# Seven-product matmuls kept to three of the six sections of a QKV projection, and twelve attention heads gathered in the other two late sections

## The chip, the cores and the metric

The kernel runs on one core of one Trainium2 chip. The metric is the device time of one execution in microseconds (us). The engines are TensorE (PE; its weight loads are shown apart as PEld), VectorE (DVE), ScalarE (ACT), GpSimd (POOL) and SyncE (SP, which issues most of the DMAs). Each engine takes its instructions strictly in the order in which they were written, and waits at one of them until what it needs is there.

## The reference

One decoder layer (DEPTH is 1) on 256 tokens of width 2048: attention with 16 heads of 128, a SwiGLU of inner width 5632, and a layer norm after each. The mixer of layer 0 is block-sparse, but with 256 tokens there is a single block of 256, so every query sees its own block alone: causal attention with a relative-position bias.

```python
def moba_mixer(x, w_qkv, w_o, rel_bias):
    q, k, v = jnp.split(x @ w_qkv, 3, axis=-1)          # 2048 -> 3 * 2048
    q, k, v = heads(q) * HEAD_DIM ** -0.5, heads(k), heads(v)
    o = moba_attention(q, k, v, rel_bias.T)              # one block: causal softmax(q k + bias) v
    return o @ w_o

def reference(...):
    x = layer_norm(ALPHA * x + moba_mixer(...), ln1_g, ln1_b)
    return layer_norm(ALPHA * x + (silu(x @ w_gate) * (x @ w_up)) @ w_down, ln2_g, ln2_b)
```

All of it is float32.

## The kernel before

**Three matmuls for one product.** Every operand is split into a high and a low part (`split`: ACT copies the high part in the fp32r format, DVE subtracts it from the source for the low part), and each product of a 128x128 by a 128x512 tile is three matmuls: high by high, high by low, low by high. Weights come from DRAM in pieces of 128 x 1024 floats (two K tiles by 512 columns, 512 KB) and are split as they arrive.

**Sections, pairs, blocks.** Each large matrix product is cut into sections of two chunks of 512 output columns. A section has 8 pairs of K tiles, and each pair is two blocks. The input projection has six sections, q0 to q5 (`QKV`); then come o0 and o1 (the attention's output projection), f0 to f10 (gate and up) and d (down). A plain pair takes two K tiles, two row halves of the tokens and two chunks: eight products, 24 matmuls, in two blocks of 12. In a section that has `comb` set, three of the eight pairs (`ST`: 1, 3, 5) are done with seven products of sums and differences in Strassen's manner: 21 matmuls, in blocks of 9 and 12. For that the weights' sums are made (`quad_sums`: four DVE additions of 128x512 for each pair) and 3.5 pieces instead of 2 are split, and differences of the two token halves (`combine_x`, tiles `xC`) stand as left operands.

**PSUM.** There are 8 banks of 128x512, handed out by a queue: `bank` takes the one that has been free longest, `give` puts a bank back. A section with `comb` holds seven sums (`acc` 1 to 7) and leaves one bank free while it runs; a plain section holds four and leaves four. At a section's end `sums_1` to `sums_3` (seven DVE operations and one of ACT) bring the seven sums together; a plain section's four are copied out.

**Attention.** One head is five steps, each put behind a block. `at_t1` transposes q and k on PE into a bank and splits them; `at_s` multiplies them into a bank, DVE adds the bias and takes the maximum (lines 453, 455), and ACT takes exponentials; `at_n` divides by the sums (reciprocal on DVE, two scalings on ACT, lines 470 and 471); `at_t2` transposes the probabilities into a bank and splits them, and splits the head's v; `at_o` multiplies by v into a bank and ACT copies the result. Heads come in four groups of four. Groups 0 to 2 run beside the projection, group 3 beside o0. Of groups 0 and 1 the result goes to DRAM (`od`) and is loaded again before the output projection (`load_o`, `split_o`).

**Order.** Nothing is scheduled: a loop writes the blocks one by one, loads and splits of a pair three to five blocks ahead of it, and before or after each block whatever `before(t, ...)` and `after(t, ...)` have put there. The six sections before are (q, k of group 0), (v of groups 0, 1), (q, k of 1), (q, k of 2), (v of 2, 3), (q, k of 3); all but q0 have `comb`. The first step of head 0 stands behind the first block of q2, each head starts 5 blocks after the one ahead of it, and its steps stand 0, 3, 6, 9 and 12 blocks behind its start, so that twelve heads spread over the 64 blocks of q2 to q5.

Of the kernel before, what the change touches and what calls it, by code (L numbers as in the profile page):

```python
# [13 lines left out]
AF = mybir.ActivationFunctionType  # L14
OP = mybir.AluOpType

P = 128
# [19 lines left out]
SKEW_D = 3  # L37
AHEAD = 3
AHEAD_Q = 5
QKV = (((0, 0), (1, 0)), ((2, 0), (2, 1)), ((0, 1), (1, 1)), ((0, 2), (1, 2)), ((2, 2), (2, 3)), ((0, 3), (1, 3)))  # L40
SQK, SV = {0: 0, 1: 2, 2: 3, 3: 5}, {1: (0, 1), 4: (2, 3)}
KEEP = 2
ST = (1, 3, 5)
WARM = 9
# [5 lines left out]
def decoder_layer(ctx: ExitStack, tc: tile.TileContext, x, xt, rel_bias, w_qkv, w_o, g1, b1, gb1,  # L50
                  w_gate, w_up, w_down, g2, b2, c_ident, c_hot, c_mask, out):
    nc = tc.nc
# [7 lines left out]
    def p4(shape, dt, name):  # L60
        return sb.tile(shape, dt, tag="p4", bufs=P4, name=name)

    def s2(shape, dt, name):
        return sb.tile(shape, dt, tag="s2", bufs=S2, name=name)

    def tiny(shape, name):
        return sb.tile(shape, F, tag="tiny", bufs=16, name=name)
# [3 lines left out]
    def bank(name):  # L71
        n = free.popleft()
        t = ps.tile([P, CW], F, tag=f"b{n}", bufs=1, name=name)
        held[id(t)] = (t, n)
        return t

    def give(*ts):
        for t in ts:
            free.append(held.pop(id(t))[1])
# [4 lines left out]
    def split(hi, lo, src):  # L84
        nc.scalar.activation(hi, src, AF.Copy)  # L85
        nc.vector.tensor_tensor(lo, src, f32(hi), op=OP.subtract)  # L86
# [83 lines left out]
    def h_lhs(kt, m):  # L170
# [1 line left out]
        return hi[:, kt % 4, m * P:(m + 1) * P], lo[:, kt % 4, m * P:(m + 1) * P]  # L172

    xC, x1C = {}, {}
    Q = [Sec(f"q{n}", [(w_qkv, 4 * i + g) for i, g in pair], 8, x_lhs, xC if n else None)
         for n, pair in enumerate(QKV)]
    WO = [Sec(f"o{i}", [(w_o, 2 * i + c) for c in range(2)], 8, o_lhs) for i in range(2)]
    NF = FF // CW
# [5 lines left out]
    def add(sec, pairs, m, chunks=None, ks=(0, 1)):  # L184
        blocks.append((sec, pairs, m, range(len(sec.chunks)) if chunks is None else chunks, ks))
        return len(blocks) - 1

    def alternate(sec, a, b):
        for p in range(a, b):
            add(sec, [p], 0)  # L190
            add(sec, [p], 1)

    for k in range(2):
        for m in range(2):
            add(Q[0], [0], m, ks=[k])
    alternate(Q[0], 1, 8)
    for s in Q[1:]:
        alternate(s, 0, 8)
    alternate(WO[0], 0, 8)
    k = 8 - SKEW_WO  # L200
# [6 lines left out]
    k = DN.npair - SKEW_D  # L207
# [7 lines left out]
    first, last = {}, {}  # L215
# [15 lines left out]
    order = []  # L231
    for s in [*Q, *WO, *FU, DN]:
        for p in range(s.npair):
            if s is Q[0] and not p:
                continue
            f = first[s.name, p]
            if s.comb is None:
                todo = [(start[s.name, p], "plain")]
            elif p in ST:
                a = 4 if s in Q or (s is FU[1] and p == 1) else 6  # L240
                todo = [(f - a, "sums"), (f - a + 1, "raw"), (f - a + 2, "low")]
# [137 lines left out]
    grp = {}  # L379

    def new_qk(g):
        grp[g] = {n: p4([P, 2, CW], F, f"{n}{g}") for n in "qk"}
        return grp[g]

    def first_qk(m):
        t = new_qk(0) if m == 0 else grp[0]
        nc.scalar.activation(t["q"][:, m, :], Q[0].acc[m, 0], AF.Copy)
        nc.vector.tensor_copy(t["k"][:, m, :], Q[0].acc[m, 1])
        give(Q[0].acc[m, 0], Q[0].acc[m, 1])


    def sums_1(s, t):
# [36 lines left out]
    att = {}  # L429
# [35 lines left out]
    def at_n(h):  # L465
        sc, sm = att[h]
        rs = tiny([P, 2], "rs")
        nc.vector.tensor_scalar(rs, sm, 1e-30, None, op0=OP.max)
        nc.vector.reciprocal(rs, rs)
        nc.scalar.activation(sc[:, :2 * P], sc[:, :2 * P], AF.Identity, scale=rs[:, 0:1])  # L470
        nc.scalar.activation(sc[:, 2 * P:], sc[:, 2 * P:], AF.Identity, scale=rs[:, 1:2])

    def at_t2(h):
        sc, _ = att[h]
        b = bank("t2")
        for i, o in enumerate((2 * P, 0, P)):
            nc.tensor.transpose(out=b[:, i * P:(i + 1) * P], in_=sc[:, o:o + P], identity=ident)
        hi, lo = s2([P, 3 * P], R, "pth"), s2([P, 3 * P], R, "ptl")
        split(hi, lo, b[:, :3 * P])
        give(b)  # L480
        vs = [s2([P, 2, P], R, f"v{i}") for i in "hl"]
        split(*vs, grp[h // 4, "v"][:, :, h % 4 * P:(h % 4 + 1) * P])
        att[h] = [hi, lo, *vs]

    def at_o(h):
        g, j = divmod(h, 4)
# [27 lines left out]
    def att_steps(g):  # L514
        steps = []
        for a in (4 * g, 4 * g + 2):
            b = a + 1
            one = [[(at_t1, a)], [(at_t1, b)], [(at_s, a)], [(at_s, b), (at_n, a)],
                   [(at_n, b), (at_t2, a)], [(at_t2, b)], [(at_o, a)], [(at_o, b)]]
            if g == 3:  # L520
                one = [one[0] + one[1], one[2], one[3], one[4][:1], one[4][1:], one[5], one[6] + one[7]]
            steps += one
        return steps
# [156 lines left out]
    def before(t, f, *a):  # L680
        pre.setdefault(t, []).append((f, a))

    def after(t, f, *a):
        post.setdefault(t, []).append((f, a))
# [6 lines left out]
    def at_sums(s, f, *a):  # L691
        t = last[s.name, 1]
        after(first[s.name, ST[-1]] + 1, f, *a, 1)
        after(t - 1, f, *a, 2)
        after(t, f, *a, 3)

    for m in range(2):
        after(last["q0", m], first_qk, m)
    for n in SV:
        at_sums(Q[n], v_sums, n)  # L700
    for g in range(4):
        if g:
            at_sums(Q[SQK[g]], qk_sums, g)
        t0 = first["q2", 0] + 20 * g if g < 3 else first["o0", 0]
        before(t0 - 2, load_bias, g)
        if g == 3:
            for n, step in enumerate(att_steps(g)):
                for f, h in step:
                    after(t0 + n, f, h)
            continue  # L710
        for j in range(4):
            for f, n in ((at_t1, 0), (at_s, 3), (at_n, 6), (at_t2, 9), (at_o, 12)):
                after(t0 + 5 * j + n, f, 4 * g + j)
        if g < 2:
            after(first["o0", 2 * g] - 5, load_o, g)
        after(max(first["o0", 2 * g] - 3, t0 + 28), split_o, g)
    after(last["o0", 0] - 6, reload_x)
    for m in range(2):
        for c in range(2):
# [19 lines left out]
    t = dn_t[0][0] - 32  # L739
# [5 lines left out]
    for i in range(NF):  # L745
        t = last[f"f{i}", 1]
# [10 lines left out]
    for i in range(NF):  # L757
        t = first["d", 2 * i]
# [14 lines left out]
    s = Q[0]  # L773
# [8 lines left out]
    for k in range(2):  # L782
        split_x(0, slice(k, k + 1))
        for c in range(2):
            hi, lo = s.pieces[0, c]
            split(hi[:, k, :], lo[:, k, :], s.raws[0, c][0][:, k, :])
    n = 0
# [59 lines left out]
```

## Time and profile before

| what | value |
|---|---|
| median of 3 runs | 1128.29 us (1127.83 to 1129.36) |
| the profiled execution's own time | 1129.13 us |
| its span (first to last instruction) | 1127.0 us |
| PE busy / PEld busy / DVE busy / ACT busy | 98% / 80% / 77% / 52% |
| stretch of q1 | 51.9 to 93.4 us of the span |
| stretch of q2 to q5, with twelve heads | 93.4 to 303.8 us |
| stretch of o0, with the last group of heads | 303.8 to 357.5 us |
| a stretch of the seven-product gate and up sections | 435 to 700 us |

Times in the trace count from the span's start. A busy share is the time in which an engine had an instruction in work. Matmuls overlap in the pipeline: one lasts 0.39 us in the rows, and the next starts 0.227 us after it, so PE can be 100% busy and a stall shows as less than that. The stretches above are read from the starts of the first matmuls of q1, q2, o0 and o1.

### The profile page before, as it was taken

Reading aid. Unit: us, or ns where it says so; the run is one execution under the profiler, and the core shown is the slowest. Engines: PE = TensorE matmul, PEld = TensorE weight load, DVE = VectorE, ACT = ScalarE, POOL = GpSimd, SP = SyncE. Lnnn points to the kernel's source line nnn. Section 1 sums busy time; section 2 is a strip of 40 time slices with the busy share of each in tenths; the row PEclk is TensorE's granted clock in tenths of the full one; section 3 lists DMA queues with packets and bytes.
Section 4 is the critical chain, followed back from the end, with each engine's and each line's share of the span. In section 5 each row is a group of like instructions: output and inputs, shape, how many; then the busy total and the mean of one; then the engine's idle time right before and its main releaser. Section 6 shows DMA issues by size and latency. Waiting matters only on the chain.

```text
span 1127.0 us, 13641 instructions
## 1 busy us (share of the span) xinstructions
PE 1099.1 (98%) x5004; PEld 904.6 (80%) x5004; DVE 866.9 (77%) x1124; ACT 589.3 (52%) x782; POOL 10.3 (1%) x16
## 2 busy tenths in 40 slices
PE   9999889998999999999999999999999999999995
PEld 6888778777888887888888888888888888888884
DVE  6898687878767768988988988988988646665446
ACT  6564556555566555745655655655656534354420
POOL 0000000000000000000000000000000000000001
PEclk9999999999999999999999999999999999999998
DMA  9665445545665726756646656656659584577511
GB/s 340 210 226 186 162 155 199 173 149 180 231 224 168 300 92 224 256 195 221 230 179 226 228 175 233 227 171 237 220 187 333 185 333 180 204 300 280 205 38 75
DMA packets 66323, 234.91 MB, mean 208 GB/s; under 512 B 7568, under 2 KB 8016, under 8 KB 66256
## 3 DMA queue, kind: packets, MB, share of 16 engines
q1 hardware_dynamic: 63488, 224.06, 56.2%
q10 hardware_dynamic: 2160, 7.87, 1.7%
q0 software_dynamic: 608, 2.12, 0.6%
q8 instruction: 39, 0.64, 0.2%
q14 instruction: 28, 0.23, 0.1%
HBM read 224.03 MB, written 9.99 MB: 208 GB/s over the span
## 4 chain that ended last, share of the span: by engine, by line
PE 80%; DVE 11%; ACT 4%; issue 2%; DMA 1%; SPq 0%; POOL 0%; ACTq 0%; DVEq 0%; POOLq 0%
PE acc_f L308 12%; PE acc_f L310 12%; PE acc_f L309 12%; PE acc_d L373 7%; PE acc_d L376 7%; PE acc_d L372 7%; PE acc_q L308 3%; PE acc_q L310 3%; PE acc_q L309 3%; PE acc_o L372 2%; PE acc_o L376 2%; PE acc_o L373 2%; DVE wl_q L86 2%; PE acc_q L373 1%; PE acc_q L376 1%
## 5 line engine op out<-in xcount | busy, mean ns | idle before, releaser
L86 DVE TENSOR_TENSOR wl_d<-r_d,wh_d 128x1024 fp32r<-128x1024 f32 x88 | 104.4, 1222 | 71.5 <-ACT wh_d L85 51.8
L86 DVE TENSOR_TENSOR wl_f<-r_f,wh_f 128x1024 fp32r<-128x1024 f32 x116 | 135.1, 1219 | 16.1 <-ACT wh_f L85 15.8
L372 PE MATMUL acc_d<-wh_d,hh 128*128 128x512 f32 x352 | 137.0, 389 | 0.0
L373 PE MATMUL acc_d<-wl_d,hh 128*128 128x512 f32 x352 | 136.9, 389 | 0.0
L85 ACT ACTIVATE wh_d<-r_d 128x1024 fp32r<-128x1024 f32 x88 | 90.7, 1057 | 75.3 <-DMA r_d<-in_w_down 44.1
L85 ACT ACTIVATE wh_f<-r_f 128x1024 fp32r<-128x1024 f32 x116 | 115.6, 1049 | 10.6 <-DMA r_f<-in_w_up 5.2
L308 PE MATMUL acc_f<-wh_f,x1h 128*128 128x512 f32 x300 | 116.9, 390 | 0.0
L310 PE MATMUL acc_f<-wh_f,x1l 128*128 128x512 f32 x300 | 116.7, 389 | 0.0
L309 PE MATMUL acc_f<-wl_f,x1h 128*128 128x512 f32 x300 | 116.7, 389 | 0.0
L376 PE MATMUL acc_d<-wh_d,hl 128*128 128x512 f32 x352 | 99.9, 389 | 0.0
L86 DVE TENSOR_TENSOR wl_q<-r_q,wh_q 128x1024 fp32r<-128x1024 f32 x64 | 75.7, 1221 | 24.1 <-ACT wh_q L85 23.6
L85 ACT ACTIVATE aq<-t 128x1024 fp32r<-128x1024 f32 x45 | 47.5, 1056 | 64.1 <-DVE t L272 60.7
L372 PEld LDWEIGHTS acc_d<-wh_d,hh 128*128 128x128 f32 x352 | 66.1, 188 | 13.8
L376 PEld LDWEIGHTS acc_d<-wh_d,hl 128*128 128x128 f32 x352 | 66.1, 188 | 13.7
L373 PEld LDWEIGHTS acc_d<-wl_d,hh 128*128 128x128 f32 x352 | 66.1, 188 | 13.7
L310 PEld LDWEIGHTS acc_f<-wh_f,x1l 128*128 128x128 f32 x300 | 56.3, 188 | 11.7
L308 PEld LDWEIGHTS acc_f<-wh_f,x1h 128*128 128x128 f32 x300 | 56.3, 188 | 11.7
L309 PEld LDWEIGHTS acc_f<-wl_f,x1h 128*128 128x128 f32 x300 | 56.3, 188 | 11.6
L85 ACT ACTIVATE wh_q<-r_q 128x1024 fp32r<-128x1024 f32 x64 | 64.1, 1048 | 2.1 <-DMA r_q<-in_w_qkv 2.1
L308 PE MATMUL acc_q<-wh_q,xh 128*128 128x512 f32 x150 | 61.1, 407 | 0.0
L86 DVE TENSOR_TENSOR aq<-t,aq 128x1024 fp32r<-128x1024 f32 x45 | 54.8, 1219 | 6.0 <-ACT aq L85 5.9
L310 PE MATMUL acc_q<-wh_q,xl 128*128 128x512 f32 x150 | 59.0, 393 | 0.0
(268 smaller groups left out, 2407.4 us busy)
## 6 DMA issues: line engine op xcount, KB each, us to landing
r_q<-in_w_qkv SPq DMA_DIRECT2D x94, 512.0 KB, 4.2
r_f<-in_w_gate SPq DMA_DIRECT2D x88, 512.0 KB, 4.1
r_f<-in_w_up SPq DMA_DIRECT2D x88, 512.0 KB, 4.9
r_d<-in_w_down SPq DMA_DIRECT2D x88, 512.0 KB, 6.0
r_o<-in_w_o SPq DMA_DIRECT2D x32, 512.0 KB, 4.4
hd<-hT ACTq DMA_DIRECT2D x9, 512.0 KB, 5.3
hT<-hd SPq DMA_DIRECT2D x9, 512.0 KB, 3.6
bias<-rows POOLq DMA_DIRECT2D x4, 512.0 KB, 4.8
```

The costliest lines, as they stand in the source:

```text
L85: nc.scalar.activation(hi, src, AF.Copy)
L86: nc.vector.tensor_tensor(lo, src, f32(hi), op=OP.subtract)
L308: nc.tensor.matmul(a, lh, rh, start=start, stop=False)
L309: nc.tensor.matmul(a, lh, rl, start=False, stop=False)
L310: nc.tensor.matmul(a, ll, rh, start=False, stop=stop)
L372: nc.tensor.matmul(a, lh, hi[:, k, :], start=kt == 0, stop=False)
L373: nc.tensor.matmul(a, lh, lo[:, k, :], start=False, stop=False)
L376: nc.tensor.matmul(s.acc[m, c], ll, hi[:, k, :], start=False, stop=kt == nk - 1)
```

## The change

Three sections (q1, q2, q3) keep seven products, and q4 and q5 become plain ones with eight, like q0. The fourth and fifth sections change places, so that the v of groups 2 and 3 is made in q3 and q, k of group 2 in q4. Groups 0 to 2 start at the first block of q4 (and not of q2), a head every 2.5 blocks (and not every 5); the steps stand 0, 3, 5, 7 and 10 blocks behind a head's start, with the splits of v now a step of their own (`at_v`, 8). The two scalings of `at_n` go from ACT to DVE. Group 3 stays beside o0; there its two splits of v per pair of heads stand together behind `at_t2` of the second head. `first_qk` becomes `qk_evac`, which any plain section uses.

```diff
-QKV = (((0, 0), (1, 0)), ((2, 0), (2, 1)), ((0, 1), (1, 1)), ((0, 2), (1, 2)), ((2, 2), (2, 3)), ((0, 3), (1, 3)))
-SQK, SV = {0: 0, 1: 2, 2: 3, 3: 5}, {1: (0, 1), 4: (2, 3)}
+QKV = (((0, 0), (1, 0)), ((2, 0), (2, 1)), ((0, 1), (1, 1)), ((2, 2), (2, 3)), ((0, 2), (1, 2)), ((0, 3), (1, 3)))
+SQK, SV = {0: 0, 1: 2, 2: 4, 3: 5}, {1: (0, 1), 3: (2, 3)}
+SEVEN = (1, 2, 3)
...
-    Q = [Sec(f"q{n}", [(w_qkv, 4 * i + g) for i, g in pair], 8, x_lhs, xC if n else None)
+    Q = [Sec(f"q{n}", [(w_qkv, 4 * i + g) for i, g in pair], 8, x_lhs, xC if n in SEVEN else None)
...
+    def qk_evac(g, m):
+        t = new_qk(g) if m == 0 else grp[g]
+        a = Q[SQK[g]].acc
+        nc.scalar.activation(t["q"][:, m, :], a[m, 0], AF.Copy)
+        nc.vector.tensor_copy(t["k"][:, m, :], a[m, 1])
+        give(a[m, 0], a[m, 1])
...
-        nc.scalar.activation(sc[:, :2 * P], sc[:, :2 * P], AF.Identity, scale=rs[:, 0:1])
-        nc.scalar.activation(sc[:, 2 * P:], sc[:, 2 * P:], AF.Identity, scale=rs[:, 1:2])
+        nc.vector.tensor_scalar(sc[:, :2 * P], sc[:, :2 * P], rs[:, 0:1], None, op0=OP.mult)
+        nc.vector.tensor_scalar(sc[:, 2 * P:], sc[:, 2 * P:], rs[:, 1:2], None, op0=OP.mult)
...
-                   [(at_n, b), (at_t2, a)], [(at_t2, b)], [(at_o, a)], [(at_o, b)]]
+                   [(at_n, b), (at_t2, a)], [(at_t2, b), (at_v, a), (at_v, b)], [(at_o, a)], [(at_o, b)]]
...
-        t0 = first["q2", 0] + 20 * g if g < 3 else first["o0", 0]
+        t0 = first["q4", 0] + 10 * g if g < 3 else first["o0", 0]
...
-            for f, n in ((at_t1, 0), (at_s, 3), (at_n, 6), (at_t2, 9), (at_o, 12)):
-                after(t0 + 5 * j + n, f, 4 * g + j)
+            for f, n in ((at_t1, 0), (at_s, 3), (at_n, 5), (at_t2, 7), (at_v, 8), (at_o, 10)):
+                after(t0 + 5 * j // 2 + n, f, 4 * g + j)
...
-        after(max(first["o0", 2 * g] - 3, t0 + 28), split_o, g)
+        after(max(first["o0", 2 * g] - 3, t0 + 18), split_o, g)
```

How it moves instructions is seen at two places. In these rows `t` is a transpose's bank, `lg` the bank of the logits, `acc_q_n` a sum of a section, and the first number is the place on the engine.

On PE before, in q2: the first transposes of probabilities (line 477), then one block of nine matmuls (three products), then the transposes of the next head's q and k (line 436). While this section runs one bank is free, so `t_1146` and `t_1167` are the same bank.

```order
525 L477 MATMUL t_1146<-ident,sc 128x128 x3
526 L308 MATMUL acc_q_1_941<-gq,xh_72 128x512
527 L309 MATMUL acc_q_1_941<-gq,xh_72 128x512
528 L310 MATMUL acc_q_1_941<-gq,xl_73 128x512
529 L308 MATMUL acc_q_2_882<-gq,xh_72 128x512
530 L309 MATMUL acc_q_2_882<-gq,xh_72 128x512
531 L310 MATMUL acc_q_2_882<-gq,xl_73 128x512
532 L308 MATMUL acc_q_3_921<-uq,xeh 128x512
533 L309 MATMUL acc_q_3_921<-uq,xeh 128x512
534 L310 MATMUL acc_q_3_921<-uq,xel 128x512
535 L436 MATMUL t_1167<-ident,q_504 128x128 x2
536 L436 MATMUL t_1167<-ident,k_505 128x128 x2
```

On PE now, the same two steps (lines 479 and 438), in q4, with the block that follows them and the next head's logits.

```order
875 L479 MATMUL t_1756<-ident,sc 128x128 x3
876 L438 MATMUL t_1769<-ident,q_504 128x128 x2
877 L438 MATMUL t_1769<-ident,k_505 128x128 x2
878 L373 MATMUL acc_q_0_0_1544<-wh_q_4_0_1668,xh_72 128x512
879 L374 MATMUL acc_q_0_0_1544<-wl_q_4_0_1669,xh_72 128x512
880 L373 MATMUL acc_q_0_1_1545<-wh_q_4_1_1674,xh_72 128x512
...
889 L377 MATMUL acc_q_0_1_1545<-wh_q_4_1_1674,xl_73 128x512
890 L451 MATMUL lg<-qkh 128x256
```

The two steps now stand in one place, behind one block, and take two different banks out of the four that a plain section leaves.

On DVE before, in q3: the end of a section's sums (lines 407 to 409), splits of a seven-product pair (`aq`, `bq`), the two small operations of `at_n`, and the splits of the next plain pair.

```order
174 L407 TENSOR_TENSOR k_1206<-acc_q_5_917,k_1206 128x512
175 L408 TENSOR_TENSOR k_1206<-acc_q_5_917,k_1206 128x512
176 L409 TENSOR_TENSOR k_1206<-acc_q_3_921,k_1206 128x512
177 L86 TENSOR_TENSOR aq<-t_1275,aq 128x1024
178 L86 TENSOR_TENSOR bq<-t_1276,bq 128x1024
179 L468 TENSOR_SCALAR rs<-sm 128x2
180 L469 RECIPROCAL rs<-rs 128x2
181 L86 TENSOR_TENSOR wl_q_2_0_1369<-r_q_2_0_1366,wh_q_2_0_1368 128x1024
```

On DVE now, in q4: a plain pair's two splits, `at_n` with its two scalings (lines 472, 473), and the next head's `at_s` (455 to 461).

```order
198 L87 TENSOR_TENSOR wl_q_4_0_1669<-r_q_4_0_1666,wh_q_4_0_1668 128x1024
199 L87 TENSOR_TENSOR wl_q_4_1_1675<-r_q_4_1_1672,wh_q_4_1_1674 128x1024
200 L470 TENSOR_SCALAR rs<-sm 128x2
201 L471 RECIPROCAL rs<-rs 128x2
202 L472 TENSOR_SCALAR sc<-sc,rs 128x256
203 L473 TENSOR_SCALAR sc<-sc,rs 128x128
204 L455 ISA sc,mx<-lg,bias_1501 128x256
205 L455 ISA mx 128x1
206 L457 ISA sc,mx<-lg,bias_1501 128x128
207 L457 ISA mx 128x1
208 L461 TENSOR_SCALAR nm<-mx 128x2
```

No sums of a seven-product pair stand between a head's steps any more; the two scalings have come to this queue from ACT's.

## Rows read from the trace of the kernel before

**Rows 1.** The page's busy times: us, share of the span, instructions.
```profile
span 1127.0 us, 13641 instructions
PE 1099.1 (98%) x5004; PEld 904.6 (80%) x5004; DVE 866.9 (77%) x1124; ACT 589.3 (52%) x782; POOL 10.3 (1%) x16
```
**Rows 2.** Stretches: length, busy us and instructions by engine, clock, DMA share, GB/s.
```profile
51.90:93.40 41.50, 41.50 (x185) 34.37 (x184) 37.13 (x44) 24.64 (x29) 0.80 (x1) 1.00 0.61 216
93.40:303.80 210.40, 198.07 (x952) 162.42 (x951) 168.75 (x279) 119.24 (x208) 2.25 (x3) 0.98 0.53 178
303.80:357.50 53.70, 53.70 (x279) 45.45 (x278) 36.95 (x72) 34.48 (x65) 0.00 (x0) 1.00 0.57 196
435.00:700.00 265.00, 265.00 (x1193) 219.09 (x1191) 232.59 (x271) 151.61 (x176) 0.00 (x0) 1.00 0.62 218
```
**Rows 3.** Waits of PE, 93.5 to 303.8: total us, times, longest.
```profile
PE t L436 <- DVE ptl L86: 6.5, 5, 2.4
PE t L477 <- DVE mx L455: 3.0, 4, 1.8
PE acc_q L308 <- DVE ptl L86: 2.8, 1, 2.8
```
**Rows 4.** PE's timeline at one wait: start us, us, instruction, idle before it.
```profile
124.66 0.39 PE L310 MATMUL acc_q<-uq,xel 128*128 128x512 f32 x1
127.41 0.44 PE L436 MATMUL t<-ident,q 128*128 128x128 f32 x2 [2.36 <-DVE ptl L86]
...
128.36 0.63 PE L309 MATMUL acc_q<-aq,xdh 128*128 128x512 f32 x1
128.79 0.63 PE L310 MATMUL acc_q<-aq,xdl 128*128 128x512 f32 x1
```
**Rows 5.** The stretches around two waits, columns as in rows 2.
```profile
122.00:135.00 13.00, 10.19 (x41) 8.07 (x41) 8.11 (x16) 7.33 (x14) 0.00 (x0) 0.87 0.50 176
262.00:270.00 8.00, 6.10 (x21) 4.90 (x22) 7.26 (x13) 3.13 (x7) 0.00 (x0) 0.79 0.50 147
```
**Rows 6.** DVE's groups, 93.4 to 303.8: busy us, mean ns, idle before.
```profile
L86 DVE TENSOR_TENSOR wl_q<-r_q,wh_q 128x1024 fp32r<-128x1024 f32 x38 | 44.8, 1221 | 20.6 <-ACT wh_q L85 20.6
...
L86 DVE TENSOR_TENSOR qkl<-t,qkh 128x512 fp32r<-128x512 f32 x12 | 8.2, 685 | 1.1 <-ACT qkh L85 1.1
...
L86 DVE TENSOR_TENSOR ptl<-t,pth 128x384 fp32r<-128x384 f32 x11 | 6.1, 552 | 1.5 <-ACT pth L85 1.4
L453 DVE CUSTOM_DVE_ANT_0 sc<-lg,bias 128x256 f32<-128x256 f32 x12 | 5.0, 419 | 0.8 <-PE lg L449 0.8
...
L86 DVE TENSOR_TENSOR vl<-v,vh 128x256 fp32r<-128x256 f32 x11 | 4.6, 415 | 0.0
L455 DVE CUSTOM_DVE_ANT_0 sc<-lg,bias 128x128 f32<-128x128 f32 x12 | 3.4, 285 | 0.0
...
L468 DVE TENSOR_SCALAR rs<-sm 128x2 f32<-128x2 f32 x12 | 2.0, 163 | 0.0
```
**Rows 7.** ACT's two scalings of `at_n`, 93.4 to 303.8, columns as in rows 6.
```profile
L470 ACT ACTIVATE sc<-sc,rs 128x256 f32<-128x256 f32 x12 | 6.1, 510 | 39.2 <-DVE rs L469 39.2
...
L471 ACT ACTIVATE sc<-sc,rs 128x128 f32<-128x128 f32 x12 | 4.6, 387 | 0.0
```
**Rows 8.** Two lines of the source, whole span: ns min/median/max, first and last start.
```profile
L571 DVE TENSOR_SCALAR y<-y,mv,rstd x8: 540/542/547, 395.7 to 409.0; 128x512 f32<-128x512 f32 x8
L388 DVE COPY k<-acc_q x2: 684/685/686, 51.1 to 54.0; 128x512 f32<-128x512 f32 x2
```
**Rows 9.** DMA issues: queue, count, KB each, median us to landing.
```profile
bias<-rows POOLq DMA_DIRECT2D x4, 512.0 KB, 4.8
...
od<-o ACTq DMA_DIRECT2D x2, 512.0 KB, 3.9
o<-od SPq DMA_DIRECT2D x2, 512.0 KB, 5.0
```

More of the change, by code (lines that the diff above doesn't have):

```diff
@@ L383, in new_qk @@
         return grp[g]
[L385 to L389, printed above, removed]
+    def qk_evac(g, m):
[4 more added lines that the diff above has]
+        give(a[m, 0], a[m, 1])
     def sums_1(s, t):
@@ L480, in at_t2, with at_v @@
         give(b)
+        att[h] = [hi, lo]
+    def at_v(h):
         vs = [s2([P, 2, P], R, f"v{i}") for i in "hl"]
         split(*vs, grp[h // 4, "v"][:, :, h % 4 * P:(h % 4 + 1) * P])
-        att[h] = [hi, lo, *vs]
+        att[h] += vs
     def at_o(h):
@@ L695, in at_sums @@
         after(t, f, *a, 3)
-    for m in range(2):
-        after(last["q0", m], first_qk, m)
     for n in SV:
@@ L701, in decoder_layer @@
     for g in range(4):
-        if g:
-            at_sums(Q[SQK[g]], qk_sums, g)
-        t0 = first["q2", 0] + 20 * g if g < 3 else first["o0", 0]
+        s = Q[SQK[g]]
+        if s.comb is not None:
+            at_sums(s, qk_sums, g)
+        else:
+            for m in range(2):
+                after(last[s.name, m], qk_evac, g, m)
+        t0 = first["q4", 0] + 10 * g if g < 3 else first["o0", 0]
         before(t0 - 2, load_bias, g)
```

## The prediction

> **What bounds the kernel now.** I began with the page's busy times [rows 1]: PE is busy 98% of the span, so any gain has to come out of PE's gaps or PE's work. Then the stretches [rows 2], which say where the gaps are. In q1 (seven products, no heads) PE is busy for all of 41.50 us, at a clock of 1.00, though DVE is busy 37.13 us, 89%. In the gate and up sections, which have the same seven products, PE has no gap in 265 us and DVE is at 88%. In o0 (plain, with four heads) PE has no gap either. Only q2 to q5, seven products and heads together, lose: PE is idle for 210.40 - 198.07 = 12.3 us, at a mean clock of 0.98.
>
> The waits there [rows 3] are ten, 6.5 + 3.0 + 2.8 = 12.3 us in sum, so they are all of it. None is a wait for a weight. The transposes of line 436 wait for `ptl`, those of line 477 for `mx`, once a section's sum waits for `ptl`: each time PE wants to write a bank and DVE has not finished reading what the head ahead left in it. With seven sums held there is one bank for all heads, and the order's rows show two uses of it one block of nine matmuls apart. That makes a free bank, not DVE's load, the thing that PE waits for.
>
> **What the waits cost in full.** A wait also empties the pipeline: a matmul's row is 0.39 us, while q1 has 183 matmuls (5 x 24 + 3 x 21) in 41.50 us, 0.227 us each; so each of the ten costs some 0.16 us more, 1.6 us together. And behind the two longest, 2.4 and 2.8 us, the matmuls last 0.63 us and start 0.43 us apart [rows 4], TensorE's lower level (1.2 GHz in place of 2.4). Around them the granted clock is 0.87 over 13 us and 0.79 over 8 us [rows 5]: (0.13 x 13) + (0.21 x 8) = 3.4 us. In all 12.3 + 1.6 + 3.4 = **17.3 us**.
>
> A second account checks it. In o0 192 matmuls take 43.5 us, so the 18 head steps that PE does there cost 53.70 - 43.5 = 10.2 us, 0.57 each. In q2 to q5 4 x 183 matmuls and 46 steps would take 166.0 + 26.1 = 192.1 of the 210.40 us [rows 2]: 18.3 us lost.
>
> **The change, part by part.**
>
> *Eight products in q4 and q5.* Six pairs get three matmuls more: 18 x 0.227 = **+4.1 us** of PE, on the path. DVE loses for each pair four additions and 1.5 splits, and the sums at two section ends; that is off the path and I count nothing for it.
>
> *Banks.* q4 and q5 hold four sums and leave four banks. By the order, a bank's next use now stands two or three blocks behind the step that filled it, and one where q5 takes over from q4; before, it was one block in each of the two kinds of step that wait. So all ten waits should go, with what hangs on them: **-17.3 us**. q2 and q3 have no heads and become copies of q1, which had no wait.
>
> *Heads at twice the rate.* PE's head steps are the same in number; five of them now fall into o0, where two did. DVE's work in q4 and q5: 32 splits of 1.221 us are 39.1; a head has `qkl` 0.685, `ptl` 0.552, `vl` 0.415, the two bias-and-maximum operations 0.419 and 0.285, three small ones at 0.163, 2.8 us [rows 6]; four copies are 2.7 [rows 8]. To this come the two scalings, which the trace doesn't show on DVE. Their bounds: no less than the small operation's 0.163 each, no more than the 0.542 of the same operation on 512 columns [rows 8]; between these by columns, 0.35 and 0.26, an estimate, 0.61 together. ACT loses 0.510 + 0.387 [rows 7]. So 12 x 3.4 + 39.1 + 2.7 = 83 us in 87.1 + 43 x 0.57 = 111.6 us: 75%. o0 had 69% and q1 89% without a wait. Even at the upper bound for the scalings it is 80%. I take nothing for them.
>
> The steps' distances: `at_n` is two blocks behind `at_s` and `at_t2` two more. Four blocks are 4 x 12 x 0.227 = 10.9 us; the work between is 0.7 for the maxima, two exponentials of the shapes of the scalings (0.9), the small ones and the new scalings, some 3 us. Behind the waiting `at_n` on DVE stand the next pair's splits, which PE needs three blocks (8.2 us) later; the two splits take 2.4.
>
> *Moved DMAs.* Bias loads on POOL's queue stand five blocks (13.6 us) ahead of their use and land in 4.8. Group 1's store on ACT's queue moves to four blocks ahead of its load on SP's, 10.9 us for 3.9; the load takes 5.0 and its split stands two blocks (5.4 us) behind, three more ahead of its use [rows 9]. SP may wait at that load; behind it stand o0's weights of the third pair, whose splits come no sooner. Nothing, with up to 3 us if that cover failed.
>
> *Where it gets tight.* The first blocks of o0: DVE has there the last heads' `at_n`, the copies of q5, two splits of `o` and the transposes of group 3, whose logits come one block later instead of three. I put **+0.7 us** there, between 0 and 3.
>
> *The sum.* By waits -17.3 + 4.1 = -13.2. By stretches: q2 and q3 83.0, q4 and q5 111.6, o0 with three steps more 55.4; 250.0 against 264.1 is -14.1. The middle, -13.7, with +0.7 is **-13.0**. The profiled execution took 1129.13 us, so 1116.1; the median of the runs is 0.84 lower, which gives **1115.3 us**.
>
> **A rule against it.** DVE's share is 80% through q2 to q5 [rows 2]; the change splits this into 89% without heads and 75% with them. The Trainium skill (Perfetto Trace Analysis, Optimization Strategy) says that stages bound by different engines may gain from being interleaved; by that the old order was the better one, and the change would bring nothing but its 4.1 us of matmuls or more. The trace differs: where they are mixed PE waits, and where the heavier share runs alone it doesn't.
>
> **Rivals.**
>
> *DVE falls behind where seven products run alone.* That is the mechanism for such a rule: two sections more in a row at DVE's highest share, and its backlog reaches PE. It decides when a section needs more than 41.5 us of DVE, 4.4 above q1's 37.1. If DVE idled in q2 and q3 for the 20% that it did in q2 to q5, a section would take 46.4 us: 2 x 4.9 = +9.8, 1125 us. Against it: ten gate and up sections in a row. Chance 0.05.
>
> *Half of the waits return in q4, q5 or o0.* For it: two heads' steps now often stand behind one block, and DVE and ACT take them in order. 17.3 / 2 on top: 1124 us. Chance 0.10.
>
> *Slower.* The waits come from the heads' chain and not from the bank: DVE gets to `ptl` late because of its queue. Then four banks cure nothing, 17.3 us stay, and 4.1 come on top: 1132 us. Twelve heads would have to wait 1.1 us each for no gain, 1.3 for a loss that shows. For it: the waits' releaser is always DVE. Against it: in o0 the same chain ran beside plain sections without a wait. Chance 0.05.
>
> *More than forecast.* Steps that stand together save PE the change between head and section; if each of some 20 steps that now follow another saved 0.1 us (an estimate, from 0.57 us for a step alone), and o0 stayed clean: -16, 1112 us. Chance 0.07.
>
> **How the numbers follow.** The forecast has 0.73. Its own range is 1113 to 1118.5, from 0 and 3 us in the tight place and the two accounts. Runs of this kernel differ by 0.1%, so I call 0.2% (2.3 us) the least that can be told from no change. For 8 in 10 the range takes in the better case and the nearer part of the half return: 1111.5 to 1120.5. All cases but the slow one are faster: 0.94, with 0.02 for the same and 0.04 for slower.
>
> **What would show it.** In the profile after, q2 and q3 should take 41.5 us each without a gap in PE; the waits of transposes for `ptl` and `mx` should be gone from q4 and q5; the clock should be 1.00 throughout; o0 should start near 288 us of the span and not at 303.8; and DVE should be near 75% in q4 and q5. The prediction is wrong if PE waits there for `qkl`, `sc` or weights (the chain or the queue), if q2 or q3 show a gap (DVE's backlog), or if o0's stretch is longer than 56 us.

## The result and the profile after

The changed kernel takes 1114.5 us (median of 4 runs, 1114.33 to 1115.11); the kernel before, beside it, 1128.27 us (4 runs, 1127.83 to 1129.36). The ratio is 0.9877, 95% interval 0.986 to 0.9895: 13.8 us faster. The forecast was 1115.3 us, in 1111.5 to 1120.5. The profiled execution took 1114.35 us, of which the span is 1112.6.

The page's busy times, which answer to [rows 1]:

```profile
PE 1097.0 (99%) x5022; PEld 906.9 (82%) x5022; DVE 845.2 (76%) x1110; ACT 571.8 (51%) x740; POOL 10.3 (1%) x16
```

The stretches q1, then q2 and q3, then q4 and q5, then o0, with the columns of [rows 2]:

```profile
51.90:93.40 41.50, 41.50 (x185) 34.38 (x184) 36.95 (x45) 26.57 (x31) 0.00 (x0) 1.00 0.62 203
93.40:176.30 82.90, 82.90 (x368) 68.66 (x367) 68.27 (x79) 38.57 (x42) 0.80 (x1) 1.00 0.63 209
176.30:287.00 110.70, 110.70 (x590) 94.54 (x589) 74.84 (x174) 58.77 (x119) 2.25 (x3) 1.00 0.57 186
287.10:343.50 56.40, 55.61 (x293) 47.00 (x293) 40.70 (x85) 37.00 (x69) 0.00 (x0) 1.00 0.55 187
```

Where [rows 2] had 210.40 us for q2 to q5 with 12.3 us of gaps, there are now 82.9 + 110.7 = 193.6 us without one, at a clock of 1.00: 16.8 us less. o0 takes 56.4 us against 53.7 and so gives 2.7 of it back. Together that is 14.1 us of the 14.4 by which the span is shorter.

The view of PE's waits, 50 to 360 us, has one row, where [rows 3] had three with ten waits:

```profile
PE t L438 <- DVE k L390: 0.8, 1, 0.8
```

It stands behind o0's first block, as the timeline there shows:

```profile
290.27 1.22 DVE L87 TENSOR_TENSOR wl_o<-r_o,wh_o 128x1024 fp32r<-128x1024 f32 x1
...
291.08 0.27 PE L438 MATMUL t<-ident,k 128*128 128x128 f32 x1
291.41 0.68 DVE L390 COPY k<-acc_q 128x512 f32<-128x512 f32 x1
...
292.15 0.33 PE L438 MATMUL t<-ident,k 128*128 128x128 f32 x1 [0.79 <-DVE k L390]
```

DVE copies the last of q5's sums into `k` behind a split of `w_o`. The first three transposes of group 3's first head have gone into their bank without a wait; the fourth reads the half of `k` that this copy writes. So it waits for data, and not for a bank.

The scalings that moved to DVE, from the view of DVE's groups, 176.3 to 343 us (busy us, mean ns, idle before); on ACT they took 510 and 387 ns [rows 7]:

```profile
L472 DVE TENSOR_SCALAR sc<-sc,rs 128x256 f32<-128x256 f32 x16 | 5.7, 354 | 0.6
...
L473 DVE TENSOR_SCALAR sc<-sc,rs 128x128 f32<-128x128 f32 x16 | 4.5, 281 | 0.0
```

### The profile page after: what moved, and what is told of

It reads as the page before. It is cut to its first block, busy times and chain, and to the rows that moved or that the text cites. A ratio compares the mean times of both kernels' runs of the same rounds, so it can differ in the third digit from the quotient of the medians.

```text
span 1112.6 us, 13662 instructions
## 1 busy us (share of the span) xinstructions
PE 1097.0 (99%) x5022; PEld 906.9 (82%) x5022; DVE 845.2 (76%) x1110; ACT 571.8 (51%) x740; POOL 10.3 (1%) x16
## 4 chain that ended last, share of the span: by engine, by line
PE 93%; DVE 3%; ACT 2%; issue 1%; DMA 1%; SPq 0%; POOL 0%; ACTq 0%; POOLq 0%; DVEq 0%
PE acc_f L311 12%; PE acc_f L309 12%; PE acc_f L310 12%; PE acc_d L377 7%; PE acc_d L373 7%; PE acc_d L374 7%; PE acc_q L311 4%; PE acc_q L309 4%; PE acc_q L310 4%; PE acc_q L373 4%; PE acc_q L374 4%; PE acc_q L377 4%; PE acc_o L373 2%; PE acc_o L377 2%; PE acc_o L374 2%; PE lg L451 1%
## 5 line engine op out<-in xcount | busy, mean ns | idle before, releaser
L87 DVE TENSOR_TENSOR wl_q<-r_q,wh_q 128x1024 fp32r<-128x1024 f32 x76 | 89.6, 1221 | 11.9 <-ACT wh_q L86 11.1
L86 ACT ACTIVATE aq<-t 128x1024 fp32r<-128x1024 f32 x39 | 41.3, 1059 | 85.2 <-DVE t L273 82.1
L86 ACT ACTIVATE wh_q<-r_q 128x1024 fp32r<-128x1024 f32 x76 | 75.9, 1048 | 2.3 <-DMA r_q<-in_w_qkv 2.1
L373 PE MATMUL acc_q<-wh_q,xh 128*128 128x512 f32 x184 | 73.9, 402 | 0.0
L374 PE MATMUL acc_q<-wl_q,xh 128*128 128x512 f32 x184 | 72.0, 391 | 0.9 <-DVE wl_q L87 0.9
```

The costliest lines, as they stand in the source:

```text
L373: nc.tensor.matmul(a, lh, hi[:, k, :], start=kt == 0, stop=False)
L374: nc.tensor.matmul(a, lh, lo[:, k, :], start=False, stop=False)
```

## The experiments

Each edit below shows the lines that matter, not the whole of it. The theory to be tested is the prediction's (the bank theory): PE waited for the one spare bank and not for DVE's load, and the four spare banks beside plain sections cure that. The rival (the chain theory) is its slower case: DVE comes late to a head's pieces because of what stands ahead of them in its queue. The kernel before was timed beside the runs again, at 1129.4 us (e1 to e4), 1129.05 (e5 to e8) and 1129.32 (e9 to e12); each ratio below is to the one beside it. Beside the changed kernel it took 1128.27, so a difference of about 1 us between runs of different groups tells nothing.

**e1 and e2: the changed kernel with fewer spare banks.** Three banks (e1) or two (e2) are kept from the heads between the first block of q4 and that of o0.

```
+    def hold(n):
+        kept.extend(free.popleft() for _ in range(n))
+    def release():
+        free.extend(kept)
+    before(first["q4", 0], hold, 3)      # 2 in e2
+    before(first["o0", 0], release)
```

> The changed kernel, with three PSUM banks laid aside from the first block of q4 to the end of q5, so that the heads there have one bank, as beside seven products; DVE's work is the same. If the wait was for a free bank, waits come back, more than before since steps stand closer: within five blocks PE waits for the copy behind ov (0.4 plus a hand-over), the maxima behind lg (0.7), ov's copy again and the split behind t2 (0.5 + 0.55), some 3.7 us for two heads at the least, 22 us in all, 1130 to 1150. If the wait came from the heads' chain on a loaded DVE, nothing changes: 1113.5 to 1116.

> As the run with one bank, with two banks laid aside, so that the heads have two. Bank theory: two uses of a bank have another step between them, ov and t2 are read while lg and t1 run; some waits of 0.3 to 1 us remain, 1115 to 1121. Chain theory: 1113.5 to 1116.

e1: 1140.31 us, 1.0097 of the kernel before (1.0082 to 1.0112). e2: 1116.94 us, 0.9893 (0.9878 to 0.9908). The first three rows of e1's waits (the kind of view of [rows 3]), and its stretch of q4 and q5:

```profile
PE t L438 <- DVE ptl L87: 5.9, 5, 1.2
PE t L438 <- DVE mx L457: 4.8, 4, 1.3
PE t L479 <- ACT o L505: 1.9, 4, 0.5
```
```profile
176.30:310.00 133.70, 117.05 (x584) 95.95 (x583) 74.83 (x171) 58.92 (x118) 2.26 (x3) 0.97 0.46 154
```

DVE does the same work as in the changed kernel, and PE has 16.7 us of gaps. With the heads gathered banks do count: with three laid aside the time is 25.8 us above the changed kernel's, with two 2.4 us.

**e3: a loaded DVE beside four banks.** Eleven adds that nobody reads stand behind the splits of six pairs of q4 and q5.

```
+        if s in Q[4:] and p in ST:
+            z = f32(zero)
+            for _ in range(11):
+                nc.vector.tensor_tensor(z, z, z, op=OP.add)
```

> The changed kernel with four banks for the heads, and 66 additions of 128x256 on DVE (0.42 us each, 27 us) added behind the splits of pairs 1, 3 and 5 of q4 and q5, on values that nothing uses: about the work that seven products would ask of DVE there. DVE's share in q4 and q5 goes from 68% to 92%. Bank theory: no more than 2 us, 1114 to 1117. Chain theory (DVE late because of its queue): the waits of before come back, 1120 to 1132.

1130.69 us, 1.0015 (1.0005 to 1.0025): the bank theory missed by 14 us. The largest rows of PE's waits:

```profile
PE t L483 <- DVE sc L477: 4.4, 1, 4.4
PE ov L503 <- DVE vl L87: 3.7, 1, 3.7
PE t L483 <- DVE qkl L87: 1.5, 1, 1.5
```

The first two, 8.1 us, are waits for data: the second transposes for the scaled `sc`, the product with v for `vl`. More banks would not have helped them. The third is a wait for a bank although four were spare: the `sc` that it transposes had been scaled 3 us before, and DVE was still reading another head's transposes (`qkl`). It stands where q5 takes over from q4, whose sums had not all been copied out.

```profile
244.20 0.28 DVE L477 TENSOR_SCALAR sc<-sc,rs 128x128 f32<-128x128 f32 x1
...
246.77 0.69 DVE L87 TENSOR_TENSOR qkl<-t,qkh 128x512 fp32r<-128x512 f32 x1 [1.53 <-ACT qkh L86]
...
247.52 0.55 PE L483 MATMUL t<-ident,sc 128*128 128x128 f32 x3 [1.46 <-DVE qkl L87]
```

**e4: plain sections alone, heads spread as before.** The kernel before with q2 to q5 plain; heads five blocks apart, scalings on ACT.

```
-    Q = [Sec(f"q{n}", [(w_qkv, 4 * i + g) for i, g in pair], 8, x_lhs, xC if n else None)
+    Q = [Sec(f"q{n}", [(w_qkv, 4 * i + g) for i, g in pair], 8, x_lhs, xC if n == 1 else None)
```

> The kernel before, with its heads spread over q2 to q5 as there and the scalings on ACT, but q2 to q5 all plain with eight products: one part of the change in four sections, without the gathering. Bank theory: the 17.3 us go, 36 matmuls come (8.2 us): 1128.3 - 17.3 + 8.2 = 1119.2, and the whole change is better than this by its 18 matmuls fewer, 4.1 us. If spreading the heads is better for PE than gathering them, less than 1116. If only gathering brings the gain, 1128 or more.

1119.28 us, 0.9914 (0.9899 to 0.9928), to the figure, and PE has no gap in q2 to q5 (the stretch shown stops 3 us ahead of o0, and the view of waits has no row):

```profile
93.40:292.00 198.60, 198.60 (x979) 166.10 (x977) 110.54 (x193) 103.29 (x185) 2.26 (x3) 1.00 0.58 188
```

But this takes two things from the heads' side at once, the shortage of banks and DVE's work on the sums of weight pieces. e5, e6, e9 and e10 part them.

**e5, e6, e9, e10: banks and DVE apart.** e5 is e4 with the `hold` of e1 from q2's first block; e6 is e4 with the adds of e3 in q2 to q5; e9 has both. e10 has four banks and nearly the same number of adds, two at a time:

```
+    def adds():
+        z = f32(zero)
+        for _ in range(2):
+            nc.vector.tensor_tensor(z, z, z, op=OP.add)
+    for n in range(64):
+        after(first["q2", 0] + n, adds)
```

> The plain, spread kernel of e4 (heads five blocks apart over four eight-product sections, DVE 56% busy in them) with three of the four spare PSUM banks held from the first block of q2 to the first of o0. If one spare bank makes the waits of the kernel before, they come back with DVE at 56%: 1122 to 1134 us. If DVE's load makes them, one bank is enough while DVE is light: 1119 to 1120.5.

> The kernel of e4 with 132 adds of 128x256 that nobody reads on DVE, 11 behind three splits of each of q2 to q5: 132 x 425 ns (the price in e3) is 56 us, which takes DVE from 110.5 of 198.6 us to about 84%; all four spare banks stay. If one spare bank made the waits of the kernel before, 1119 to 1122 us. If DVE's load made them, 1128 to 1137.

> The fourth cell of the square of e4, e5 and e6: heads spread over plain sections, the 132 adds on DVE in lumps of 11, and one spare PSUM bank. If DVE's lumps alone make the waits, as with four banks: 1133 to 1136 us. If a late DVE costs more where only one bank is spare, 1137 to 1145.

> The kernel of e4 with 128 of the same adds, two behind every block of q2 to q5 in place of lumps of 11: the same share of DVE as e6 (about 82%), four spare banks. If the share of DVE makes the waits, 1128 to 1135 us as in e6. If it is what stands ahead of a head's piece in DVE's queue at that moment, a lump of 4.7 us there and 0.85 us here, 1119 to 1122.

| heads spread, plain sections | four spare banks | one spare bank |
|---|---|---|
| DVE as it is | e4: 1119.28 | e5: 1119.47 |
| adds, eleven at a time | e6: 1134.03 | e9: 1170.63 |
| adds, two at a time | e10: 1119.31 | not run |

Against the kernel before these are 0.992 (0.9903 to 0.9936) for e5, 1.0051 (1.0036 to 1.0066) for e6, 1.0373 (1.0354 to 1.0391) for e9 and 0.9917 (0.9901 to 0.9933) for e10. One bank by itself costs nothing. Adds in lumps cost 14.8 us with four banks; with one they cost 51.2, more than either theory gave. Nearly the same load in small pieces costs nothing, though DVE is then busy 156.04 of 198.6 us, 79%:

```profile
93.40:292.00 198.60, 198.60 (x979) 166.10 (x978) 156.04 (x315) 101.13 (x183) 2.26 (x3) 1.00 0.58 186
```

e6's waits, in the view of [rows 3], are for data, so more banks don't help them:

```profile
PE lg L465 <- DVE qkl L86: 3.9, 2, 2.2
PE ov L510 <- DVE ptl L86: 3.8, 2, 2.2
PE acc_q L377 <- DVE wl_q L86: 1.4, 4, 0.4
```

The logits wait for `qkl`, the product with v for `ptl`, and four matmuls for a weight split. So DVE's share does not matter here; what matters is how much stands ahead of a head's piece when it comes. (e10 also puts the adds at other places; no run parts the size of a lump from its place.) A stretch of e9's timeline:

```profile
149.76 5.01 DVE L305 TENSOR_TENSOR zero<-zero 128x256 f32<-128x256 f32 x11
...
150.53 0.61 PE L380 MATMUL acc_q<-wh_q,xl 128*128 128x512 f32 x2
154.69 0.68 DVE L86 TENSOR_TENSOR qkl<-t,qkh 128x512 fp32r<-128x512 f32 x1
...
155.43 0.80 PE L376 MATMUL acc_q<-wh_q,xh 128*128 128x512 f32 x1 [4.29 <-DVE qkl L86]
...
158.16 0.63 PE L376 MATMUL acc_q<-wh_q,xh 128*128 128x512 f32 x1
158.58 0.63 PE L377 MATMUL acc_q<-wl_q,xh 128*128 128x512 f32 x1
...
161.33 0.39 PE L377 MATMUL acc_q<-wl_q,xh 128*128 128x512 f32 x1
161.56 0.40 PE L376 MATMUL acc_q<-wh_q,xh 128*128 128x512 f32 x1
```

The lump starts just ahead of `qkl`, which reads the heads' bank. So `qkl` is five us late, and a section's first sum, which needs that bank, waits 4.29 us. With four banks (e6) no wait of this kind is seen.

**e12: the kernel before with a light DVE.** DVE's part in the sums of weight pieces and in their splits is left out, so products 4 to 7 multiply other pieces and the output is not the layer's. PE's and ACT's instructions and the one spare bank stay.

```
+        if s in Q[2:]:                       # quad_sums: no additions
+            quad[s.name, p] = g, u, None, None
+            return
...
+            g2 = quad_g2.pop(p)              # quad_low: ACT's halves alone
+            nc.scalar.activation(a2[0], f32(g2[0]), AF.Copy)
+            nc.scalar.activation(b2[0], f32(g2[0]), AF.Copy)
```

> The kernel before with DVE's part in the sums of weight pieces and in their splits left out for q2 to q5: six instructions in each of twelve places, 62 us; products 4 to 7 take other pieces in their place, so that TensorE's and ScalarE's instructions, their order and the one spare bank stay as they were. If DVE's load makes the waits, they go with what they cost: 1129 - 12.3 - 1.6 - 3.4 = 1112 us (1111 to 1115). If the one bank makes them, they stay: 1125 to 1130.

1111.56 us, 0.9847 (0.9831 to 0.9862). q2 to q5, 210.40 us in [rows 2], take 193.80, with PE idle for 0.6 of it, beside one bank and seven products:

```profile
93.40:287.20 193.80, 193.24 (x954) 161.38 (x954) 116.53 (x212) 119.97 (x208) 2.26 (x3) 1.00 0.58 193
```

So one spare bank is not enough to make the waits, and the bank theory is refuted where it was made. The timelines of one place show how. First the kernel before, in the 9 us ahead of the wait of [rows 4]:

```profile
118.69 0.27 PE L449 MATMUL lg<-qkh,qkl 128*128 128x128 f32 x1
...
119.40 1.22 DVE L86 TENSOR_TENSOR aq<-t,aq 128x1024 fp32r<-128x1024 f32 x1
120.54 1.22 DVE L86 TENSOR_TENSOR bq<-t,bq 128x1024 fp32r<-128x1024 f32 x1
121.67 0.42 DVE L453 CUSTOM_DVE_ANT_0 sc<-lg,bias 128x256 f32<-128x256 f32 x1
...
122.55 0.51 ACT L461 ACTIVATE sc<-sc,nm 128x256 f32<-128x256 f32 x1 [2.50 <-DVE nm L459]
...
123.44 1.99 ACT L85 ACTIVATE wh_q<-r_q 128x1024 fp32r<-128x1024 f32 x2
124.52 2.36 DVE L86 TENSOR_TENSOR wl_q<-r_q,wh_q 128x1024 fp32r<-128x1024 f32 x2 [2.01 <-ACT wh_q L85]
126.80 0.55 DVE L86 TENSOR_TENSOR ptl<-t,pth 128x384 fp32r<-128x384 f32 x1
```

Then e12 at the same place:

```profile
119.24 0.27 PE L460 MATMUL lg<-qkh,qkl 128*128 128x128 f32 x1
...
119.55 0.42 DVE L464 CUSTOM_DVE_ANT_0 sc<-lg,bias 128x256 f32<-128x256 f32 x1 [2.43 <-PE lg L460]
...
122.41 2.37 DVE L86 TENSOR_TENSOR wl_q<-r_q,wh_q 128x1024 fp32r<-128x1024 f32 x2 [2.01 <-ACT wh_q L85]
124.69 0.55 DVE L86 TENSOR_TENSOR ptl<-t,pth 128x384 fp32r<-128x384 f32 x1
...
125.30 0.44 PE L447 MATMUL t<-ident,q 128*128 128x128 f32 x2 [0.56 <-DVE ptl L86]
```

In the kernel before the logits end at 118.96 us, and DVE, busy with a seven-product pair's splits (`aq` and `bq` are of its sums), comes to their maxima at 121.67, 2.7 us later. ACT waits 2.50 us for what follows from them, with the weights' splits behind it in its queue; DVE waits for those; `ptl` stands behind them. In e12, without the lump, the maxima start 0.04 us behind the logits, and PE's wait is 0.56 us in place of 2.36. ACT waits for DVE there too, 2.75 us, but its exponentials start 0.9 us behind the logits and not 3.6.

**e11: gathering alone.** The changed kernel with `SEVEN = (1, 2, 3, 4, 5)`.

> The other half of the change alone: the twelve heads gathered in q4 and q5, scaling on DVE, but seven products in all five sections, so one spare bank and the combining work of DVE beside the heads. If keeping the heads out of q2 and q3 were enough, 1108 to 1115 us. If the heads at twice the density need q4 and q5 plain, more waits than e1's, for DVE has some 40 us more there: 1140 to 1160.

1142.02 us, 1.0117 (1.0099 to 1.0135). The first two rows of its waits:

```profile
PE t L438 <- DVE mx L457: 7.7, 4, 2.9
PE t L438 <- DVE ptl L87: 3.5, 3, 1.2
```

By halves, then: plain sections alone (four of them, not two) gain 10.1 us (e4), gathering with the scalings on DVE alone loses 12.7 (e11), and the change, which has both, gains 13.8. What the move of the scalings does by itself was not tried.

**e7: the last wait.** The copies of a plain section are written ahead of the heads' steps that hang on the same block.

```
                 after(last[s.name, m], qk_evac, g, m)
+    for g in range(4):
         t0 = first["q4", 0] + 10 * g if g < 3 else first["o0", 0]
```

> The changed kernel with the two copies that empty a plain section's banks written ahead of the heads' steps that hang on the same block. The one wait of TensorE that is left, 0.8 us in the first block of o0 behind DVE's copy of k, should go: 1113.5 to 1114.2 us. If another of DVE's pieces takes its place, 1114.3 to 1115.

1114.28 us (1113.9 to 1114.41), 0.9874 (0.9859 to 0.9889). The wait shrank to 0.4 us, and the time lies between the two expectations. It can't be told from the changed kernel's time.

**e8: one step further.** q4 takes seven products, and all twelve heads run in q5.

```
-SEVEN = (1, 2, 3)
+SEVEN = (1, 2, 3, 4)
...
-            for f, n in ((at_t1, 0), (at_s, 3), (at_n, 5), (at_t2, 7), (at_v, 8), (at_o, 10)):
-                after(t0 + 5 * j // 2 + n, f, 4 * g + j)
+            for f, n in ((at_t1, 0), (at_s, 2), (at_n, 4), (at_t2, 6), (at_v, 6), (at_o, 8)):
+                after(t0 + 5 * j // 4 + n, f, 4 * g + j)
```

> The change taken one step further: q4 takes seven products too and holds no attention, all twelve heads run in q5, 1.25 blocks apart, and the attention outputs of the first two groups stay in SBUF. q4 loses 16 matmuls of 0.227 us and its refills: -3.5 to -4. By the banks alone, with four spare ones in q5, 1110.5 to 1112.5 us. If the chain of each head runs through DVE (the miss of e3), DVE's share in q5 passes 85% and waits of 5 to 15 us come: 1116 to 1126.

1130.84 us, 1.0015 (1.0005 to 1.0025), slower than either expectation. The three largest rows of PE's waits, and the stretch from q5 on:

```profile
PE t L438 <- ACT q L389: 4.0, 1, 4.0
PE t L438 <- DVE qkl L87: 3.0, 2, 1.5
PE lg L451 <- DVE mx L457: 2.2, 4, 1.3
```
```profile
218.00:310.00 92.00, 81.12 (x419) 68.25 (x418) 59.88 (x161) 47.25 (x110) 1.50 (x2) 0.91 0.36 115
```

DVE is busy 65% there, not 85%. The gaps are 10.9 us. The longest, 4.0 us, is a wait for data in o0: a transpose reads the half of `q` that ACT has not yet copied, and its bank it already has.

```profile
300.22 0.33 PE L438 MATMUL t<-ident,q 128*128 128x128 f32 x1
304.58 0.48 PE L438 MATMUL t<-ident,q 128*128 128x128 f32 x1 [4.03 <-ACT q L389]
```

In the others `t` and `lg` wait for DVE to read what earlier heads left in the banks. At this density four banks are too few for DVE's pace; whether more banks or a prompter DVE would cure it was not tried. What the clock of 0.91 over 92 us adds was not measured apart.

## Why the prediction was right, and where its reason was not

**The total** was 0.8 us off, and the terms held. The ten waits were priced at 17.3 us with refill and slow clock; e12 removes all but 0.6 us of them with little else on PE, and gains 17.8 us. q2 and q3 were put at 83.0 us and q4 and q5 at 111.6, and took 82.9 and 110.7. For o0 the sum had 55.4 us and the tight place's 0.7 on top; it took 56.4, 0.8 of it the one wait. The prediction had set more than 56 us there as a sign against it; it was passed by 0.4. The place was right, though the wait was for the copy of `k` and not for the logits. The scalings cost 0.354 and 0.281 us against the estimates of 0.35 and 0.26. DVE's share in q4 and q5 is 68%, forecast 75%: of the 32 splits that were counted 29 fall into the stretch, of the twelve `ptl` ten. In q2 and q3 it is 82%, where the prediction had q1's 89. Neither cost anything.

**The step that failed** is "That makes a free bank, not DVE's load, the thing that PE waits for". e5 has one bank and no wait; e12 has the kernel before's own bank and one wait of 0.6 us. The rows named the bank rightly as what PE wanted, but not why it was still full: DVE came late to it, behind the sums of weight pieces and their splits. The signs offered for the bank (q1 and the gate sections without a wait, with DVE at 88 to 89%) had no heads in them, so no chain that could come late; and o0, without a wait, had neither heavy lumps nor one bank, so it spoke for either.

**Why the total came right all the same.** The change takes away both factors. Of the four additions and one and a half splits that DVE loses for each pair of q4 and q5 the prediction said "I count nothing for it"; with the heads at the old distance that alone would have been enough (e12). So the total owes something to luck: the change removed a cause that its forecast had put at nothing. e6 shows what the banks alone might have left: with lumps of 4.7 us and four banks, waits that cost 14.8 us. The rival called slower had the right cause (DVE late to `ptl` by its queue), and failed only because it let the cause stay. Whether four banks would have cured the kernel before with its own lumps was not tried, since seven sums hold seven of its eight banks.

**What the banks do.** Too few of them multiply what a late DVE costs. With the heads five blocks apart one bank costs 0.2 us with a prompt DVE (e5) and 36.6 us more than four with a late one (e9 against e6). Gathered, at 2.5 blocks, one bank costs 25.8 us without any lump (e1), two cost 2.4 (e2). So the gathering needs more than one bank, though two come close to four, while the waits of the kernel before needed the lumps.

**The other rivals.** DVE did not fall behind where seven products run alone: q2 and q3 have no gap. No waits came back in q4 and q5. Heads' steps side by side may have saved something: q4 and q5 together are 0.9 us below the forecast, where that rival wanted some 2, but no run shows that this is the reason.

**The rule against it.** The Trainium skill (Perfetto Trace Analysis, Optimization Strategy) says that regimes with different busiest engines may gain from being interleaved. e4, interleaved, and the changed kernel, apart, differ by 4.8 us, of which 4.1 are the matmuls of two more plain sections, so between interleaved and apart no more than 0.7 us is left, which is not clear of the 1 us named above. Where heads were mixed with lumps PE waited (the kernel before), and without the lumps it hardly did (e12). The same section says that the same gap repeated on the engine that should be full can mean too few buffers; here that reading of [rows 3] was half the truth.

## What to carry to other kernels

When an engine waits for a buffer, look at why its reader is late before adding buffers: follow the reader's own queue back for some 10 us, since with heads five blocks apart one bank was enough for a prompt reader, and four were not enough for one that was 5 us late. (At 2.5 blocks one bank was too few for the prompt reader too.) The busy share of the reader does not show this: 79% in pieces of 0.85 us cost nothing, nearly the same work in pieces of 5 us cost 15 us. And an edit that takes away two causes says nothing of either; vary each with the other held still, as in the square of e4, e5, e6 and e9.

## What was not expected of the hardware

Two causes together cost more than their sum: one bank by itself cost 0.2 us, lumps by themselves 14.8, both together 51.4. Part of it is the clock: the granted mean for the whole span was 0.982 in e9 and 0.996 in e5. Behind the wait of 4.29 us in e9's timeline above PE's matmuls last 0.63 us and start some 0.43 us apart for 5 us (TensorE's lower level, 1.2 GHz in place of 2.4; the granted clock from 155.4 to 161.0 us is 0.58), and then 0.23 again; so a wait that long cost more than its length.
